# Low parts of weights issued later, and head outputs read back in place, in a one-step hybrid encoder

## The chip, the core and the metric

The kernel runs on one core of a Trainium2 chip. The metric is the device time of one execution in microseconds. Five engines work beside each other, each through its own instructions in order: TensorE (PE, matrix products), VectorE (DVE), ScalarE (ACT), GpSimd (POOL) and SyncE (SP), which here issues the transfers between memory and on-chip buffers.

## What is computed

One layer over 512 new frames and 32 frames of a running stream, T = 544 columns in all. Two groups of 16 heads (stick-breaking attention and RWKV-7) read one normalised input through one input projection; their outputs go through one output projection; a gated feed-forward part with a short convolution follows. Cut from the reference:

```python
xn = rms_norm(x, p['norm1_g'])
proj = xn @ p['w_in']
q, k, v, xr = jnp.split(proj, [D_SB, 2 * D_SB, 3 * D_SB], axis=-1)
...
o = stick_breaking(q, k_all, v_all, P)
o = rms_norm(o, p['sb_out_g'][:, None, :])
...
y_r, S_T, new_shift = rwkv7_mix(xr, shift0, S0, p)
x = x + jnp.concatenate([o, y_r.astype(x.dtype)], axis=-1) @ p['w_out']
f, new_conv = conv_ffn(rms_norm(x, p['norm2_g']), conv0, p)
x = x + f.astype(x.dtype)
```

The model is 2048 wide (16 blocks of 128 rows, k = 0 to 15), the feed-forward part 5632.

## The kernel before

**Products in three parts.** Each fp32 operand of a large product is split into a high part that TensorE takes at full rate (`hi`, made by a ScalarE cast) and the rest (`lo`, made by a VectorE subtraction that reads the cast). A product is then hi·hi + hi·lo + lo·hi. `products` (L376) issues this for one 128×128 weight block and both halves of the columns: four matmuls of 272 columns with the weight's high part, and then two with its low part.

**Weights.** They come in groups of four blocks (128×512 elements), in the order of a list `PLAN`. A group is loaded into one of 3 buffers `wr`, cast by ScalarE into one of 2 buffers `wh`, and VectorE writes its low part into one of 2 buffers `wl`. A group is 24 matmuls. `prefetch` (L313) issues casts, low parts and loads up to two groups ahead and is called after each block; `split` (L363) is called where TensorE takes the next group.

**Order of the work.** The kernel is emitted by a program that keeps an estimated clock for each engine (`clk`). While it emits the projection's matmuls, it emits pieces of the heads' side work between them (`tick`, threads) when their inputs should be there by this estimate. Every engine then carries out its own instructions in the order in which they were emitted. An engine whose next instruction waits does nothing else meanwhile.

**The start.** The 16 blocks of the input are transposed, normalised by VectorE (`xn`), cast by ScalarE (`xh`), and VectorE takes the low part (`xl`). The first two column blocks of the projection (8 weight groups: for each four k, one group for either block) are emitted by `first_products` in among this, for k = 0 to 3 once the loop over k has emitted k = 7, for k = 4 to 7 once it has emitted k = 11, and so on:

```python
    for kb in range(KB):
        if kb > 0:
            if kb + 1 < KB:
                x_high(kb + 1)
            x_low(kb)
        if kb % 4 == 3 and kb > 3:
            first_products(kb - 7)
```

**The projections** (about 57 to 985 us): 48 further column blocks of four groups each, with the heads' side work between the matmuls. Tiles of this side work that the text names are `XA`, `XB` (values and states of the RWKV chain), `AM`, `w` (general work tiles).

**The output projection.** A finished head's output goes to memory (`ocat`) and, once the last projection releases the input's tiles, `fetch` (L1435) reads it back into a `w` tile, from which `xh` and `xl` are made. Column blocks that are begun before all heads are done are kept as partial sums in memory (`pd`).

**The feed-forward part** (1200 us to the end) works mostly with products of pairs of column blocks, whose weights are split by another routine (`weights`).

Of the kernel before, what the change touches and what calls it, by code (L numbers as in the profile page):

```python
# [8 lines left out]
F32 = mybir.dt.float32  # L9
F32R = mybir.dt.float32r  # L10
BF16 = mybir.dt.bfloat16
AF = mybir.ActivationFunctionType
ALU = mybir.AluOpType
# [3 lines left out]
P = 128  # L17
# [4 lines left out]
T = SEQ + DEC  # L22
# [19 lines left out]
def hymba_step(ctx: ExitStack, tc: tile.TileContext, A: dict, O: dict):  # L42
# [19 lines left out]
    LAT = 140  # L62
    RATE = [0]
    clk = {e: 0.0 for e in COST}
# [26 lines left out]
    def stamp():  # L91
        return cur[0].ready() if cur[0] is not None else clk["PE"]

    def cols(ap):
        n = 1
        for d in ap.shape[1:]:
            n *= d
        return n
# [14 lines left out]
    V, G, AC = Engine(nc.vector, "DVE"), Engine(nc.gpsimd, "POOL"), Engine(nc.scalar, "ACT")  # L113
    act = AC.activation

    def dma(out, in_):
        if RATE[0]:
            n = cols(out) * out.shape[0] * 4
            clk["DMA"] = max(clk.get("DMA", 0.0), stamp(), clk["PE"]) + n / RATE[0]
            if cur[0] is not None:  # L120
                cur[0].rd["DMA"] = clk["DMA"] + 2300
        elif cur[0] is not None:
            cur[0].rd["DMA"] = max(clk["PE"], cur[0].ready()) + 3000
        nc.sync.dma_start(out, in_)

    def spawn(g, first=False):
        n = sum(th.first for th in threads)
        threads.insert(n if first else len(threads), Thread(g, first))
# [37 lines left out]
    def settle():  # L166
        if cur[0].ready() > clk["PE"]:
            yield


    FREE = {}
# [3 lines left out]
    def alloc(tag, shape, dtype=F32):  # L175
        after(FREE[tag].pop(0))
        pool, bufs, full = POOLS[tag]
        t = pool.tile(list(shape), dtype, tag=tag, name=nm(tag), bufs=bufs, padded_shape=full)
        OF[t.name] = tag
        return t  # L180

    def get(tag, shape=None, dtype=F32):
        while not FREE[tag]:
            yield
        t = alloc(tag, shape or POOLS[tag][2], dtype)
        yield from settle()
        return t
# [13 lines left out]
    def put(*ts):  # L201
        for t in ts:
            FREE[OF.pop(t.name)].append(stamp())
# [86 lines left out]
    raw_of, split_of = {}, {}  # L290
# [7 lines left out]
    def apart(j):  # L298
        return PLAN[j][3] in ("q", "x")

    def can_load(j):
        to = PLAN[j][3]
        return len(FREE.get("q", "")) > 1 if to == "q" else FREE["xh"] and len(FREE["xl"]) > 1 if to == "x" else FREE["wr"]
# [6 lines left out]
    def limit():  # L310
        return state["limit"] or len(PLAN)

    def prefetch():  # L313
        i = state["at"]
        while state["split"] < limit():
            j = state["split"]
            if j >= i + (QSPL if PLAN[j][3] else SPL) or not (apart(j) or FREE["wh"] and FREE["wl"]):
                break
            if state["dma"] <= j:
                if not can_load(j):  # L320
                    break
                load()
            if j > i and clk["PE"] < state[j]:
                break
            raw, ts = raw_of.pop(j)
            n = len(PLAN[j][1])
            hi, lo = ts or [alloc(t, [P, n, P], F32R) for t in ("wh", "wl")]
            AC.copy(hi, raw)
            V.tensor_tensor(lo, raw, hi.bitcast(F32), op=ALU.subtract)
            put(raw)  # L330
            split_of[j] = (hi, lo)
            state["split"] += 1
        while state["dma"] < limit():
            j = state["dma"]
            if j >= state["split"] + (QRAW if apart(j) else RAW) or not can_load(j):
                break
            load()

    def load():
        j = state["dma"]  # L340
        w, g, c0, to = PLAN[j]
        n = len(g)
        ts = None
        if apart(j):
            raw = alloc("q" if to == "q" else "xl", [P, 2 * T if to == "q" else T])
            if to == "q":
                t = alloc("q", QW, F32R)
                ts = [t[:, u * T:u * T + n * P] for u in range(2)]
            else:
                ts = [alloc(t, [P, T], F32R)[:, :n * P] for t in ("xh", "xl")]  # L350
            raw, ts[0], ts[1] = [t[:, :n * P].rearrange("p (k n) -> p k n", n=P) for t in [raw] + ts]
        else:
            raw = alloc("wr", [P, n, P])
        a = 0
        for b in range(1, n + 1):
            if b == n or g[b] != g[b - 1] + 1:
                dma(raw[:, a:b, :], w[g[a] * P:(g[b - 1] + 1) * P, c0:c0 + P].rearrange("(k p) n -> p k n", p=P))
                a = b
        raw_of[j] = raw, ts
        state["dma"] += 1  # L360
        state[j] = clk["DMA"] + 2300 if RATE[0] else clk["PE"]

    def split():  # L363
        j = state["at"]
        prefetch()
        state["at"] += 1
        return split_of.pop(j)

# [56 lines left out]
    xh, xl = [], []  # L425
# [183 lines left out]
    ocat = dr.tile([16, P, T], F32, name="ocat", bufs=1)  # L609
# [603 lines left out]
    def more_room():  # L1213
        yield from wait(SS[NP - 2], "done")
        yield from wait(SS[NP - 1], "products")
        am = yield from get("AM", None, F32R)
        ar = yield from get("AR", None, F32R)
        x = [am[:, :NC_ * P], am[:, NC_ * P:], ar]
        sp = [[x[u][:, g * 384:(g + 1) * 384] for u in (0, 2)] for g in range(2)]
        sp.append([x[1][:, u * 512:(u + 1) * 512] for u in range(2)])  # L1220
        ROOM.append((stamp(), sp))
# [210 lines left out]
        put(v)  # L1432

    spawn(more_room())
    def fetch(kb):  # L1435
        raw = yield from get("w")
        dma(raw[:, :T], ocat[kb])
        yield
        h = yield from get("xh", [P, T], F32R)
        l = yield from get("xl", [P, T], F32R)  # L1440
        AC.copy(h, raw[:, :T])
        V.tensor_tensor(l, raw[:, :T], h.bitcast(F32), op=ALU.subtract)
        put(raw)
        oh[kb], ol[kb] = h, l

    def head_done(kb):
# [3 lines left out]
    def fetch_all():  # L1450
        todo = list(range(KB))
        while todo:
            for kb in [k for k in todo if head_done(k)]:
                if kb not in oh:
                    if len(FREE["w"]) < 6:
                        break
                    spawn(fetch(kb))
                todo.remove(kb)
            yield
# [261 lines left out]
    for t in range(2):  # L1721
        for m in LAST:
            ps = getm("ps")
            for k in ALLK:
                if k % WN == 0 and t == 0:
                    kept[m, k] = split()
                hi, lo = kept[m, k // WN * WN]
# [410 lines left out]
    for t in range(2):  # L2138
        for k in range(KB):
            until(lambda: (k, t) in XN)  # L2140
            for u in range(2):
                if t == 0 and k % WN == 0:
                    sw[u, k] = split()
                hi, lo = sw[u, k // WN * WN]
# [192 lines left out]
    for gi, g in enumerate(GROUPS):  # L2337
        for m in range(LEAD):
            ps = banks(("ps", "pt")[n % 2], 2)
            for i in range(0, len(g), WN):  # L2340
                hi, lo = split()
                for q, k in enumerate(g[i:i + WN]):
                    j = k - g[0]
                    until(lambda: (gi, j // 2, 1) in HB)
                    h, l = [[HB[gi, j // 2, t][e][0][:, j % 2] for t in range(2)] for e in range(2)]
# [44 lines left out]
```

## Time and profile before

| | |
|---|---|
| median of 3 runs | 2658.87 us (2658.36 to 2659.29) |
| the profiled execution | 2658.17 us, of which 2656.3 us are the span from the first to the last instruction |
| TensorE busy | 2612.2 us, 98% of the span |
| VectorE, ScalarE, GpSimd busy | 1964.5 us (74%), 1361.4 us (51%), 241.8 us (9%) |
| DMA | 304.5 MB, mean 115 GB/s |
| mean granted TensorE clock | 0.996 of full speed |

Busy time is the time in which at least one instruction of the engine runs. TensorE's matmuls overlap each other, so its busy share tells where it stood still rather than how fast it ran. What an engine waited for is read from the idle time ahead of an instruction and from the semaphore that ended it.

### The profile page before, as it was taken

The page shows a single profiled execution, that of the slowest core. Times are in us where ns is not written, and L with a number is a line of the kernel's source. Part 1 is how long each engine was busy: PE and PEld are TensorE (multiplying, and loading weights), DVE is VectorE, ACT ScalarE, POOL GpSimd, SP SyncE. Part 2 cuts the span into 40 slices and gives each one's busy share as a digit, 9 for nine tenths or more (in the row PEclk, how much of TensorE's full clock was granted, in tenths as well). Part 3 has the DMA queues.
Part 4 walks back from the last instruction along what each step waited for, and adds up shares of the span by engine and source line. Part 5 has one row for each costly group of instructions (what it writes and reads, how often), then busy time and mean ns, then how long its engine had stood idle before and what let it go on. Part 6 is the DMA issues. An engine that isn't in the chain of part 4 may idle for free.

```text
span 2656.3 us, 54012 instructions
## 1 busy us (share of the span) xinstructions
PE 2612.2 (98%) x21546; PEld 2530.1 (95%) x21546; DVE 1964.5 (74%) x3589; ACT 1361.4 (51%) x2703; POOL 241.8 (9%) x609
## 2 busy tenths in 40 slices
PE   8999999999999999999999999999999999999999
PEld 7989988998889989999999999999999999999998
DVE  6676777676666755447788888888888897887887
ACT  5556666675666566435444444444444453443443
POOL 3210110111110100020010110101011000000000
PEclk9999999999999999999999999999999999999999
DMA  5222222232222243563334344443434364565653
GB/s 194 83 73 59 73 72 71 68 85 61 77 68 78 69 127 98 161 185 97 112 104 121 105 132 111 109 113 104 121 105 132 110 207 140 166 203 150 192 161 91
DMA packets 493237, 304.52 MB, mean 115 GB/s; under 512 B 45306, under 2 KB 458362, under 8 KB 492986
## 3 DMA queue, kind: packets, MB, share of 16 engines
q1 hardware_dynamic: 491706, 296.62, 38.8%
q0 software_dynamic: 1280, 4.46, 0.4%
q8 instruction: 169, 2.77, 0.4%
q14 instruction: 82, 0.67, 0.1%
HBM read 253.57 MB, written 47.43 MB: 113 GB/s over the span
## 4 chain that ended last, share of the span: by engine, by line
PE 64%; DVE 2%; ACT 1%; issue 0%; DMA 0%; SPq 0%; ACTq 0%; DVEq 0%
PE pt L216 27%; PE ps L216 27%; PE pj L216 9%; DVE q L109 1%; PE ps L220 0%; DVE w L109 0%; DVE wl L109 0%; ACT w L109 0%; ACT wh L109 0%; DVE xl L109 0%; ACT sp L109 0%; DMA cc<-in_cache_sb_v 0%; DVE sp L109 0%; ACT f L109 0%; DMA out_y_prompt<-f 0%
## 5 line engine op out<-in xcount | busy, mean ns | idle before, releaser
L216 PE MATMUL pj<-xh,wh 128*128 128x272 f32 x1868 | 537.4, 303 | 7.7 <-ACT wh L109 3.1
L216 PE MATMUL pj<-xl,wh 128*128 128x272 f32 x1868 | 511.8, 289 | 0.3 <-DVE xl L109 0.3
L109 DVE TENSOR_TENSOR q<-q,q 128x1024 f32<-128x1024 f32 (+7 forms) x463 | 471.0, 1038 | 6.4 <-ACT q L109 3.1
L216 PE MATMUL pj<-xh,wl 128*128 128x272 f32 x1868 | 444.0, 308 | 2.4 <-DVE wl L109 2.3
L216 PEld LDWEIGHTS pj<-xh,wh 128*128 128x128 f32 x1868 | 354.9, 190 | 20.6 <-issue 6.3
L216 PEld LDWEIGHTS pj<-xl,wh 128*128 128x128 f32 x1868 | 354.3, 190 | 4.0 <-issue 1.2
L109 DVE TENSOR_TENSOR wl<-wr,wh 128x512 fp32r<-128x512 f32 (+1 forms) x301 | 213.0, 709 | 192.7 <-ACT wh L109 186.0
L109 ACT CAST wr<-q 128x512 fp32r<-128x512 f32 (+1 forms) x301 | 180.3, 612 | 306.5 <-DVE q L109 216.9
L216 PEld LDWEIGHTS pj<-xh,wl 128*128 128x128 f32 x1868 | 302.7, 190 | 16.1 <-issue 4.5
L109 ACT CAST wh<-wr 128x512 fp32r<-128x512 f32 (+1 forms) x301 | 183.0, 610 | 165.5 <-PE pj L216 80.0
L216 PE MATMUL ps<-xh,q 128*128 128x272 f32 x922 | 241.2, 289 | 0.0
L216 PE MATMUL ps<-q,q 128*128 128x272 f32 x1160 | 237.5, 289 | 0.0
L216 PE MATMUL pt<-xh,q 128*128 128x272 f32 x1038 | 233.4, 288 | 0.0
L216 PE MATMUL pt<-q,q 128*128 128x272 f32 x844 | 215.7, 289 | 0.0
L109 DVE TENSOR_TENSOR q<-q,wr 128x512 fp32r<-128x512 f32 (+1 forms) x301 | 200.4, 674 | 0.5 <-ACT wr L109 0.4
L216 PEld LDWEIGHTS ps<-q,q 128*128 128x128 f32 x1160 | 180.9, 188 | 0.3 <-ACT f L109 0.3
L216 PEld LDWEIGHTS pt<-xh,q 128*128 128x128 f32 x1038 | 174.5, 188 | 0.0
L216 PEld LDWEIGHTS ps<-xh,q 128*128 128x128 f32 x922 | 165.3, 188 | 0.0
L109 ACT CAST q<-q 128x1024 fp32r<-128x1024 f32 (+5 forms) x197 | 147.5, 766 | 24.7 <-DVE q L109 19.0
L109 ACT CAST wh<-q 128x512 fp32r<-128x512 f32 (+1 forms) x190 | 114.1, 601 | 70.3 <-PE ps L216 34.4
L216 PEld LDWEIGHTS pt<-q,q 128*128 128x128 f32 x844 | 147.8, 188 | 0.0
L216 PE MATMUL pt<-xl,q 128*128 128x272 f32 x520 | 141.7, 289 | 0.0
(335 smaller groups left out, 6290.2 us busy)
## 6 DMA issues: line engine op xcount, KB each, us to landing
wr<-in_w_in SPq DMA_DIRECT2D x200, 256.0 KB
q<-in_w_ffn_up SPq DMA_DIRECT2D x84, 512.0 KB
q<-in_w_ffn_gate SPq DMA_DIRECT2D x80, 512.0 KB
q<-in_w_ffn_down SPq DMA_DIRECT2D x48, 512.0 KB
hd<-f SPq DMA_DIRECT2D x44, 272.0 KB
q<-hd SPq DMA_DIRECT2D x22, 544.0 KB
wr<-in_w_ffn_down SPq DMA_DIRECT2D x44, 256.0 KB
q<-in_w_ffn_down SPq DMA_DIRECT2D x24, 384.0 KB
```

What stands on the lines that cost most here:

```text
L109: return f(*a, **kw)
L216: nc.tensor.matmul(out, lhsT, rhs, start=start, stop=stop, skip_group_check=True)
```

## The change

**Low parts.** `prefetch` no longer emits a group's subtraction right behind its cast. The group is put on a list `HALF` with the time at which the estimated ScalarE clock has the cast done (plus 140 ns). At its next calls `prefetch` first runs `lows`, which emits the subtractions whose time the estimated TensorE clock has reached; `split` emits those that the group it hands out still lacks. The raw buffer is released with the subtraction, as before, so its next load moves with it.

**Fetch.** A head's output is read back into the `xl` tile in which its low part will stand (the subtraction then works in place); the `w` tile and the condition that six be free go. The cast and the subtraction are emitted in separate steps, when the estimated clocks of ScalarE and VectorE are not over 500 ns ahead of TensorE's.

```diff
--- before.py
+++ after.py
@@ -310,8 +310,20 @@
     def limit():
         return state["limit"] or len(PLAN)
 
+
+
+    HALF = []
+
+    def lows(need=-1):
+        while HALF and (HALF[0][0] <= need or HALF[0][4] <= clk["PE"]):
+            j, raw, hi, lo, _ = HALF.pop(0)
+            V.tensor_tensor(lo, raw, hi.bitcast(F32), op=ALU.subtract)
+            put(raw)
+            split_of[j] = (hi, lo)
+
     def prefetch():
         i = state["at"]
+        lows()
         while state["split"] < limit():
             j = state["split"]
             if j >= i + (QSPL if PLAN[j][3] else SPL) or not (apart(j) or FREE["wh"] and FREE["wl"]):
@@ -326,9 +338,7 @@
             n = len(PLAN[j][1])
             hi, lo = ts or [alloc(t, [P, n, P], F32R) for t in ("wh", "wl")]
             AC.copy(hi, raw)
-            V.tensor_tensor(lo, raw, hi.bitcast(F32), op=ALU.subtract)
-            put(raw)
-            split_of[j] = (hi, lo)
+            HALF.append((j, raw, hi, lo, clk["ACT"] + LAT))
             state["split"] += 1
         while state["dma"] < limit():
             j = state["dma"]
@@ -363,6 +373,7 @@
     def split():
         j = state["at"]
         prefetch()
+        lows(j)
         state["at"] += 1
         return split_of.pop(j)
 
@@ -1432,15 +1443,20 @@
         put(v)
 
     spawn(more_room())
+
     def fetch(kb):
-        raw = yield from get("w")
-        dma(raw[:, :T], ocat[kb])
+        l = yield from get("xl", [P, T], F32R)
+        raw = l.bitcast(F32)
+        dma(raw, ocat[kb])
         yield
         h = yield from get("xh", [P, T], F32R)
-        l = yield from get("xl", [P, T], F32R)
-        AC.copy(h, raw[:, :T])
-        V.tensor_tensor(l, raw[:, :T], h.bitcast(F32), op=ALU.subtract)
-        put(raw)
+        while clk["ACT"] > clk["PE"] + 500:
+            yield
+        AC.copy(h, raw)
+        yield
+        while clk["DVE"] > clk["PE"] + 500:
+            yield
+        V.tensor_tensor(l, raw, h.bitcast(F32), op=ALU.subtract)
         oh[kb], ol[kb] = h, l
 
     def head_done(kb):
@@ -1452,8 +1468,6 @@
         while todo:
             for kb in [k for k in todo if head_done(k)]:
                 if kb not in oh:
-                    if len(FREE["w"]) < 6:
-                        break
                     spawn(fetch(kb))
                 todo.remove(kb)
             yield
```

Where instructions move, at two places. The names are tiles with their numbers; `wl`, `wh`, `wr` are low part, high part and raw weights, `xn`, `xh`, `xl` the same of the input.

VectorE at the start of the kernel, behind the parameters' copy, before:

```order
L109 TENSOR_TENSOR wl_50_287<-wr_8_120,wh_49_286 128x512
L109 SCALAR_TENSOR_TENSOR xn_51_294<-xt_126,par_7_111,rsb_128 128x544
L109 TENSOR_TENSOR xl_53_298<-xn_51_294,xh_52_295 128x544
L109 TENSOR_TENSOR wl_55_301<-wr_9_122,wh_54_300 128x512
L109 SCALAR_TENSOR_TENSOR xn_58_308<-xt_126,par_7_111,rsb_128 128x544
L109 SCALAR_TENSOR_TENSOR xn_62_324<-xt_126,par_7_111,rsb_128 128x544
L109 TENSOR_TENSOR xl_64_328<-xn_58_308,xh_59_309 128x544
L109 SCALAR_TENSOR_TENSOR xn_65_330<-xt_126,par_7_111,rsb_128 128x544
L109 TENSOR_TENSOR xl_67_334<-xn_62_324,xh_63_325 128x544
```

VectorE at the same place of the changed kernel: behind the parameters' copy there come nine `xn` and eight `xl` without a weight between them, of which the last `xl` is the first row here.

```order
L109 TENSOR_TENSOR xl_80_358<-xn_75_348,xh_76_349 128x544
L109 TENSOR_TENSOR wl_50_287<-wr_8_120,wh_49_286 128x512
L109 TENSOR_TENSOR wl_55_300<-wr_9_122,wh_54_299 128x512
L109 SCALAR_TENSOR_TENSOR xn_87_421<-xt_126,par_7_111,rsb_128 128x544
L109 TENSOR_TENSOR xl_89_425<-xn_78_354,xh_79_355 128x544
L109 SCALAR_TENSOR_TENSOR xn_90_428<-xt_126,par_7_111,rsb_128 128x544
L109 TENSOR_TENSOR xl_92_432<-xn_87_421,xh_88_422 128x544
L109 SCALAR_TENSOR_TENSOR xn_93_435<-xt_126,par_7_111,rsb_128 128x544
L109 TENSOR_TENSOR xl_95_439<-xn_90_428,xh_91_429 128x544
L109 SCALAR_TENSOR_TENSOR xn_96_442<-xt_126,par_7_111,rsb_128 128x544
L109 TENSOR_TENSOR xl_98_446<-xn_93_435,xh_94_436 128x544
L109 TENSOR_TENSOR wl_82_386<-wr_10_124,wh_81_385 128x512
```

The low part of the first weight group (`wl_50`) stood ahead of the first `xn`, that of the second (`wl_55`) behind the first `xl`. Both now stand behind the eighth `xl`, and those of the third and fourth group (`wl_82` and the `wl_85` that follows the last row), which stood where `wl_50` and `wl_55` now stand, behind the twelfth.

VectorE in the projections, at the place that the trace of before has at about 188 to 194 us, before (`sp` and `ts` belong to the attention's side work, `TH` to the RWKV chain's):

```order
L109 COPY w_347_2227<-AM_343_2189 64x576 x2
L109 TENSOR_TENSOR sp_134_729<-w_323_2000,sp_134_729 64x512
L109 TENSOR_TENSOR wl_388_2404<-wr_342_2175,wh_387_2403 128x512
L109 COPY ts_379_2366<-ps_382_2379 128x128
L109 TENSOR_TENSOR sp_135_730<-w_358_2260,sp_135_730 64x2x128
L109 COPY XA_259_1555<-ps_390_2417 64x64
L109 TENSOR_TENSOR wl_395_2452<-wr_357_2256,wh_394_2451 128x512
L109 SCALAR_TENSOR_TENSOR XA_259_1555<-XA_259_1555,pc_183_1045,ps_397_2459 64x64 x2
```

The same stretch of the changed kernel:

```order
L109 TENSOR_TENSOR sp_134_727<-w_357_2260,sp_134_727 64x2x128
L109 SCALAR_TENSOR_TENSOR XA_258_1545<-XA_258_1545,pc_181_1029,ps_387_2413 64x64 x2
L109 TENSOR_SCALAR w_384_2395<-w_345_2185,m16_674 128x9x16
L109 SCALAR_TENSOR_TENSOR w_384_2395<-w_345_2185,m16_674,w_384_2395 128x9x16 x3
L109 TENSOR_TENSOR TH_330_2054<-TH_330_2054,pc_306_1908 128x1152
L109 TENSOR_TENSOR wl_386_2397<-wr_352_2229,wh_385_2396 128x512
L109 COPY XA_258_1545<-ps_396_2467 64x64
L109 TENSOR_TENSOR sp_134_727<-w_357_2260,sp_134_727 64x2x128
L109 TENSOR_TENSOR wl_398_2470<-wr_368_2304,wh_397_2469 128x512
```

Before, a `wl` stands between the two steps of the RWKV chain (`XA` copied, then updated) whose order is fixed; now they and the chain's other work stand ahead of the two `wl`, or between them. In the order in which the instructions are emitted, all but one of the 200 groups of the projections had their low part 29 large matmuls ahead of its first use (that use counted). Now 33 have it 5 ahead, that is at the `split` itself, 32 have it 11, 88 have it 17 and 47 have it 23 ahead; all eight groups of the start have it 5 ahead. All other counts (matmuls, side work) are the same; 12 fewer transfers are issued, 6 of them because 5 instead of 8 column blocks of the output projection go through memory as partial sums.

## Rows read from the trace of the kernel before

**Rows 1.** The page of the profiled execution, its first part: busy us of each engine (share of the span) and its instructions.

```profile
PE 2612.2 (98%) x21546; PEld 2530.1 (95%) x21546; DVE 1964.5 (74%) x3589; ACT 1361.4 (51%) x2703; POOL 241.8 (9%) x609
```

**Rows 2.** Busy time by stretch. Columns: the stretch in us and its length; then busy us (and instructions) of PE, PEld (weight loads of TensorE), DVE, ACT and POOL; the granted TensorE clock (1.00 is the upper of its two levels, 2.4 GHz; 0.50 the lower, 1.2 GHz); mean share of the DMA engines; GB/s. The stretches: one near the start, the projections with heads beside them, the output projection, the paired products of the feed-forward part.

```profile
21.50:31.70 10.20, 8.54 (x32) 7.50 (x33) 9.38 (x15) 5.90 (x10) 7.89 (x16) 0.50 0.94 339
...
100.00:1100.00 1000.00, 975.72 (x8642) 903.82 (x8642) 668.49 (x1463) 623.75 (x1408) 111.93 (x271) 1.00 0.27 79
1100.00:1300.00 200.00, 198.70 (x1564) 196.99 (x1563) 127.92 (x213) 85.90 (x168) 28.47 (x43) 1.00 0.50 150
1300.00:2500.00 1200.00, 1200.00 (x9543) 1199.83 (x9543) 981.23 (x1568) 534.03 (x912) 72.15 (x194) 1.00 0.46 131
```

**Rows 3.** Who waited for whom between 100 and 1100 us, of TensorE's waits and of VectorE's: the engine, the tile that it wrote and the line, what it waited for; us in total, times, longest.

```profile
PE ps L216 <- DVE XA L109: 6.6, 8, 1.8
PE ps L216 <- DVE XB L109: 3.2, 5, 1.2
...
PE pj L216 <- DVE wl L109: 2.3, 3, 1.3
...
DVE wl L109 <- ACT wh L109: 139.2, 110, 3.6
```

**Rows 4.** The timeline between 189 and 195 us, of VectorE, of ScalarE and of TensorE: start us, us, engine, line, operation, out<-in, shapes, count, and in brackets the idle time ahead and what ended it.

```profile
189.83 0.21 DVE L109 COPY XA<-ps 64x64 f32<-64x64 f32 x1
192.73 1.23 DVE L109 TENSOR_TENSOR wl<-wr,wh 128x512 fp32r<-128x512 f32 x1 [2.69 <-ACT wh L109]
193.88 0.58 DVE L109 SCALAR_TENSOR_TENSOR XA<-XA,pc,ps 64x64 f32<-64x64 f32 x2
...
190.30 1.35 ACT L109 COPY AM<-AR 64x576 f32<-64x576 f32 x2
...
192.07 0.62 ACT L109 CAST wh<-wr 128x512 fp32r<-128x512 f32 x1
...
194.62 0.46 PE L216 MATMUL ps<-XA,AM 128*128 128x128 f32 x2 [1.81 <-DVE XA L109]
```

**Rows 5.** The first and the last of the 15 TensorE stalls of over 0.25 us between 100 and 1100 us that have a VectorE wait of a `wl` in the few microseconds ahead of them, as in rows 4: each time VectorE's row and TensorE's.

```profile
182.71 0.69 DVE L109 TENSOR_TENSOR wl<-wr,wh 128x512 fp32r<-128x512 f32 x1 [2.04 <-ACT wh L109]
...
184.50 0.55 PE L220 MATMUL ps<-ident,w 128*128 128x128 f32 x3 [0.75 <-DVE w L109]
...
893.25 0.69 DVE L109 TENSOR_TENSOR wl<-wr,wh 128x512 fp32r<-128x512 f32 x1 [3.54 <-ACT wh L109]
...
894.90 0.49 PE L216 MATMUL ps<-ru,w 128*128 128x128 f32 x2 [0.36 <-DVE AM L109]
```

**Rows 6.** Two short stretches, columns as in rows 2.

```profile
195.50:198.90 3.40, 3.40 (x19) 3.40 (x18) 3.33 (x5) 1.46 (x4) 1.82 (x1) 0.52 0.19 57
...
393.50:396.90 3.40, 3.40 (x18) 3.31 (x18) 2.03 (x5) 1.04 (x4) 1.09 (x3) 0.52 0.20 56
```

**Rows 7.** The timeline of VectorE at the start, columns as in rows 4.

```profile
20.19 0.74 DVE L109 TENSOR_TENSOR wl<-wr,wh 128x512 fp32r<-128x512 f32 x1
...
22.33 0.72 DVE L109 TENSOR_TENSOR xl<-xn,xh 128x544 fp32r<-128x544 f32 x1 [0.71 <-ACT xh L109]
22.98 0.68 DVE L109 TENSOR_TENSOR wl<-wr,wh 128x512 fp32r<-128x512 f32 x1
23.58 1.47 DVE L109 SCALAR_TENSOR_TENSOR xn<-xt,par,rsb 128x544 f32<-128x544 f32 x2
...
33.25 0.71 DVE L109 TENSOR_TENSOR xl<-xn,xh 128x544 fp32r<-128x544 f32 x1
34.56 1.29 DVE L109 TENSOR_TENSOR wl<-wr,wh 128x512 fp32r<-128x512 f32 x2 [0.60 <-ACT wh L109]
```

**Rows 8.** The timeline of TensorE at the start: the first matmul, the first with a low part, one matmul of each of two weight blocks that follow each other at the lower clock and of two that lie four blocks apart at the upper, the last of the second weight group, the last of the eighth and the first of the ninth.

```profile
22.35 0.59 PE L216 MATMUL pj<-xh,wh 128*128 128x272 f32 x1 [1.70 <-ACT xh L109]
...
23.96 0.65 PE L216 MATMUL pj<-xh,wl 128*128 128x272 f32 x2
...
30.02 0.43 PE L216 MATMUL pj<-xh,wh 128*128 128x272 f32 x1
...
31.38 0.43 PE L216 MATMUL pj<-xh,wh 128*128 128x272 f32 x1
...
33.58 0.41 PE L216 MATMUL pj<-xh,wl 128*128 128x272 f32 x2
...
50.45 0.29 PE L216 MATMUL pj<-xh,wh 128*128 128x272 f32 x1
...
53.47 0.29 PE L216 MATMUL pj<-xh,wh 128*128 128x272 f32 x1
...
53.98 0.41 PE L216 MATMUL pj<-xh,wl 128*128 128x272 f32 x2
56.77 0.39 PE L216 MATMUL pj<-xh,wh 128*128 128x272 f32 x1 [2.38 <-ACT w L109]
```

**Rows 9.** The timeline of ScalarE at the start.

```profile
33.91 1.14 ACT L109 CAST wh<-wr 128x512 fp32r<-128x512 f32 x2
36.58 0.65 ACT L109 CAST xh<-xn 128x544 fp32r<-128x544 f32 x1 [1.53 <-DVE xn L109]
...
51.15 0.62 ACT L109 CAST wh<-wr 128x512 fp32r<-128x512 f32 x1 [2.36 <-PE pj L216]
```

## Prediction

> **What bounds the kernel now.** I read the page first: TensorE is busy in 2612.2 of 2656.3 us [rows 1], so it stands still for 44.1 us, and no change of order can give back more than these and what a lowered clock costs. The table by stretch says where they are [rows 2]: none between 1300 and 2500 us, 1.3 us between 1100 and 1300, 24.3 us between 100 and 1100 us, where the heads' side work runs between the projection's matmuls. Most of the rest lies in the first 57 us. The changed routine works in the projections, the output projection and the start; the feed-forward part, which takes over half the time, has nothing to gain.
>
> Then the waits. VectorE sat idle for 139.2 us, 110 times, in front of a `wl` whose cast ScalarE had not done [rows 3]. By itself that costs nothing, as VectorE is busy in two thirds of that stretch. It costs where something that TensorE wants stands behind. TensorE's largest waits there are on `XA` (6.6 us) and `XB` (3.2 us), not on `wl` (2.3 us) [rows 3], and one place shows how [rows 4]: VectorE copies an `XA` at 189.83 us, waits 2.69 us for a cast that ScalarE reaches at 192.07, behind copies of `AM`, does two `wl`, and updates `XA` at 193.88. TensorE, which wants this `XA`, stands still for 1.81 us. Of the stalls over 0.25 us in the stretch, 15 have such a `wl` wait shortly ahead; they add up to 13.7 us, the first is 0.75 and the last 0.36 us long [rows 5].
>
> One us after that stall, and once more at 393.5 us, the granted clock is at its lower level for 3.4 us, 0.52 in the rows, and comes back [rows 6]; at half speed that costs 1.7 us each time.
>
> **The change part by part.** The sum is made against the profiled execution's 2658.17 us, 0.7 under the median of the three runs.
>
> *Waits removed.* If the `wl` stand behind finished casts, the 13.7 us go, and the two spells of low clock, 3.4 us: **−17.1**. Bounds: nothing, if ScalarE is later than the estimate that defers them; 24.3 + 3.4 = 27.7 if every stall of the stretch goes.
>
> *Low parts that come too late.* Of 200 groups, 33 now have their `wl` emitted at the `split`, 5 matmuls ahead of its use. A large matmul takes 0.126 us (24 of them in 53.47 − 50.45 = 3.02 us [rows 8]), so TensorE is there after 4 × 0.126 = 0.50 us. A `wl` takes 0.69 us [rows 5], and VectorE is in the middle of something: a mean instruction of that stretch is 668.5/1463 = 0.46 us [rows 2], half of it 0.23. That leaves 0.69 + 0.23 − 0.50 = 0.42 us of stall, 33 × 0.42 = **+13.9**. The 32 with 11 matmuls have 1.26 us for the same 0.92 and cost nothing by this, and the rest less so. Bounds: nothing, where VectorE is ahead of TensorE, as it can be once nothing blocks it; and 33 × 1.27 = 42 us if each waits as long as a `wl` waited until now (139.2/110 [rows 3]). I take the middle value, since its parts are all read off rows; behind each late `wl` wait the side work's next VectorE steps.
>
> *The start.* Here the order of VectorE tells more than the stalls. Before, the first `wl` is done ahead of the first `xn`, at 20.19 us, and the second at 22.98 [rows 7]; TensorE begins at 22.35 and takes its first low part at 23.96 [rows 8]. Now nine `xn` and eight `xl` stand ahead of both. The eighth `xl` ended at 33.25 + 0.71 = 33.96 us [rows 7]; without the two `wl` in front it ends 1.3 us earlier, at 32.7, and the first `wl` at 33.3. TensorE issues four matmuls with the first high part and then waits for that, some nine us, where before it had the first two groups done at 33.99 [rows 8].
>
> From there the start is a chain, since each pair of groups waits for the next block of VectorE's `xl`. Casts need the `wh` of the group two back, as the rows of ScalarE show (a cast waits 2.36 us for TensorE at 51.15 [rows 9]), and the casts of a pair stand ahead of the next `xh` (33.91, then 36.58 [rows 9]). The steps: first pair, 44 matmuls left from 33.3 on, 5.5 us, done at T1 = 38.8. Then the fourth group's cast 0.57 [rows 9], `xh` 0.65 [rows 9], three `xl` of 0.65 and two `xn` of 0.74 in turn [rows 7], `wl` 0.69: 5.3 us, during which TensorE has four matmuls. Second pair 5.5 us: T2 = T1 + 10.9 = 49.7, with 0.1 for hand-overs. Third pair: cast 0.57, `xh` 0.65, `xl`, `xn`, `xl`, `xl` 2.7, `wl` 0.69, so 4.6, and 5.5 again: T3 = 59.9. The fourth pair has no `xl` ahead of it: 48 matmuls, 6.0 us, done at 65.9. Before it was done at 53.98 + 0.41 = 54.39 [rows 8]. That is 11.5 us later, at full clock throughout. TensorE stands still for about 9, 4.8 and 4.1 us in it. In the kernel before the clock was at 0.50 from 21.5 to 31.7 us [rows 2], after TensorE had waited 1.70 us at 22.35 and more before [rows 8], and stalls of under 2 us were followed by spells of 3.4 us [rows 6]. I count one such spell, 1.7 us, for each of the three: 5.1. Together **+16.6**. Bounds: with everything but the first wait hidden, eight groups less four matmuls from 33.3 on at 0.126 us end at 57.0, +2.6; with all of the first three pairs at the lower clock, where a matmul takes 1.36/6 = 0.227 us (31.38 − 30.02 [rows 8]), 132 × 0.10 = 13.3 on top of 11.5, +25. The 2.38 us ahead of the ninth group [rows 8] stay: they wait for the first two blocks' results to be taken away. Nothing behind can absorb the delay, since TensorE is full.
>
> *Raw buffers and loads.* A buffer is released with its `wl`, so the load of the group three later starts some two us later. It has two groups of 3 us in hand, and the DMA engines are at 0.27 [rows 2]: nothing. At the start the fourth group's load starts at 33.3 and is wanted at 38.8: hidden by the first pair.
>
> *Fetch and partial sums.* Twelve transfers and three additions on VectorE fewer, `w` tiles free earlier, casts and subtractions spread out. TensorE stands still for 1.3 us between 1100 and 1300 us [rows 2]. I count nothing, within 2 us either way; the new waits of `fetch` hold no tile that TensorE waits for.
>
> Sum: 2658.2 − 17.1 + 13.9 + 16.6 = **2671.6 us**.
>
> **A page against the rows.** The Trainium skill's page "Perfetto Trace Analysis" (Identifying the Most-Contended Engine) says that matmul busy time does not tell how far TensorE is from its limit and that weight-load busy time does. Weight loads were busy for 903.8 of 1000 us in the projections [rows 2], so by it the room there is 96 us, not 24.3. The rows speak for less: the stretch has 8642 matmuls in 1000 us, 0.116 us each, against 1200/9543 = 0.126 us where TensorE never waits [rows 2]. They are on average smaller there, which makes for shorter weight loads beside as much work. I keep 24.3 for the sum; the rule is the last of the rivals.
>
> **The rivals.**
>
> *VectorE runs ahead* (the faster side). Without 139 us of waits in its queue VectorE reaches late `wl` before TensorE does, so they cost nothing, and the other stalls go too: 2658.2 + 16.6 − 27.7 = 2647.1; with the 17.1 alone 2657.7. For it: 139.2 us are two fifths of VectorE's idle time there [rows 2, 3]. Against it: VectorE's other waits are for ScalarE and TensorE and remain. It decides for faster once waits removed less late ones exceed 16.6 + 5.3 = 21.9 us. 0.17 (0.10 faster, 0.07 level).
>
> *The start hides the rest.* The second and third wait don't occur and only +2.6 and one spell of low clock remain: 2658.2 + 4.3 − 3.2 = 2659.3. It needs the `xh` casts to pass ahead of the weights' casts; ScalarE's order has them behind. 0.08 (0.02 faster, 0.06 level).
>
> *Late low parts become the bound.* At 1.27 us each, 42 instead of 13.9: 2699.7. For it: the 33 lie in clusters, where each delays what the next one needs. 0.11.
>
> *Room inside the busy time.* If waits hide in TensorE's busy time as well, the share of `wl` in the visible stalls, 13.7/24.3, of 96.2 us is 54 us instead of 13.7: 2631. 0.04, and it is the page's rule that would have this.
>
> **How the numbers follow.** My case, a start that costs 12 to 25 us and projections that come out about level, has 0.60; its own range is 2662 to 2688. 0.2%, 5.3 us, is about what a measurement of this kernel tells from no change. Slower: 0.60 + 0.11 = 0.71. Level: 0.07 + 0.06 = 0.13. Faster: 0.10 + 0.02 + 0.04 = 0.16. The range 2653 to 2690 leaves out the last rival, the lower half of the first and most of the third, under 0.2.
>
> **What the changed profile would show.** TensorE's first low-part matmul at about 33 us instead of 23.96, waits on `wl` at some 44 and 54 us, and the ninth group at about 68 us or later instead of 56.77. VectorE's wait of `wl` on `wh` far below 139 us, waits on `XA` and `XB` smaller, waits of TensorE on `wl` well above 2.3 us between 100 and 1100 us. No stall in the feed-forward part. The prediction is wrong if the first low part comes early, if the second and third waits are missing, or if the `wl` waits of TensorE in the projections stay at 2 us.

## The result, and the profile after

The changed kernel takes 2691.18 us (median of 4 runs, 2689.76 to 2692.75) against 2658.61 us (4 runs): 1.0122 times the time before, 95% interval 1.0105 to 1.014. That is 32.6 us more; the prediction had 13.4 more. The direction was right, the time lies just above its range. The profiled execution has 2692.75 us and a span of 2691.0, 34.7 us more than the span before; the places below are read in it.

The page's first part: busy us of each engine, its share and its instructions.

```profile
PE 2618.1 (97%) x21546; PEld 2536.8 (94%) x21546; DVE 1961.7 (73%) x3584; ACT 1360.1 (51%) x2701; POOL 246.0 (9%) x609
```

TensorE is busy for 5.9 us more than in [rows 1], although it issues the same 21,546 matmuls, and it stands still for 72.9 us instead of 44.1. The second is new waiting; the first goes with more time at the lower clock (below), though no run separates it.

Who waited for whom between 100 and 1100 us, TensorE and VectorE; columns as in [rows 3].

```profile
DVE w L109 <- ACT w L109: 69.4, 56, 3.8
DVE sp L109 <- ACT sp L109: 42.8, 38, 5.4
...
PE pj L216 <- DVE wl L109: 26.9, 24, 2.8
DVE wl L109 <- ACT wh L109: 19.7, 21, 3.0
```

The change did what it says: VectorE's waits of `wl` on `wh` went from 139.2 us [rows 3] to 19.7. But VectorE did not get ahead by it. It now stands in front of the heads' own steps, `w` and `sp`, whose ScalarE halves are not done (69.4 and 42.8 us), and the `wl` stand behind these. By themselves these waits are not the loss: the fastest run below has them as well (74.0 us on `w`). The same two rows of the kernel before:

```profile
DVE w L109 <- ACT w L109: 37.8, 33, 3.4
...
DVE sp L109 <- ACT sp L109: 18.8, 22, 2.1
```

TensorE's waits for VectorE's `XA` and `XB` have left the list; in their place are 26.9 us on `wl`, which were 2.3.

By stretch, columns as in [rows 2]: three low-clock places of the start, two in the projections, the projections as a whole, one right behind the last projection, and the feed-forward part.

```profile
19.90:37.00 17.10, 6.18 (x28) 5.23 (x28) 15.41 (x24) 7.54 (x13) 9.70 (x18) 0.52 0.85 294
...
44.00:51.00 7.00, 4.67 (x20) 4.67 (x21) 4.91 (x8) 1.17 (x3) 0.00 (x0) 0.54 0.26 76
...
57.50:64.50 7.00, 5.54 (x24) 5.54 (x25) 1.99 (x4) 0.66 (x2) 4.87 (x26) 0.56 0.28 80
...
214.50:221.50 7.00, 5.15 (x23) 5.15 (x24) 4.00 (x6) 2.05 (x5) 1.53 (x4) 0.56 0.31 87
...
416.80:420.20 3.40, 3.40 (x18) 3.40 (x17) 1.88 (x4) 0.62 (x1) 0.07 (x1) 0.52 0.52 150
...
100.00:1100.00 1000.00, 967.38 (x8557) 896.50 (x8557) 668.73 (x1469) 625.14 (x1411) 120.36 (x284) 0.99 0.27 76
...
1018.00:1030.00 12.00, 9.42 (x55) 8.30 (x56) 6.76 (x15) 9.70 (x23) 0.93 (x2) 0.72 0.25 67
...
1320.00:2520.00 1200.00, 1198.03 (x9521) 1197.29 (x9521) 979.60 (x1563) 531.79 (x908) 74.11 (x202) 1.00 0.46 130
```

Between 100 and 1100 us TensorE has 8.3 us less of busy time than in [rows 2], its weight loads 7.3 less; since the changed kernel comes later, the stretch also holds 85 matmuls fewer. The 1200 us of the feed-forward part, which had no idle time in [rows 2], have 2 us of it.

TensorE at the start, columns as in [rows 8]: the last matmul ahead of each of three waits, the first behind it, and the first of the ninth group.

```profile
23.31 0.43 PE L216 MATMUL pj<-xl,wh 128*128 128x272 f32 x1
33.60 0.82 PE L216 MATMUL pj<-xh,wl 128*128 128x272 f32 x2 [9.85 <-DVE wl L109]
...
41.48 0.29 PE L216 MATMUL pj<-xl,wh 128*128 128x272 f32 x1
46.34 0.82 PE L216 MATMUL pj<-xh,wl 128*128 128x272 f32 x2 [4.57 <-DVE wl L109]
...
54.63 0.29 PE L216 MATMUL pj<-xl,wh 128*128 128x272 f32 x1
58.96 0.82 PE L216 MATMUL pj<-xh,wl 128*128 128x272 f32 x2 [4.04 <-DVE wl L109]
...
75.55 0.39 PE L216 MATMUL pj<-xh,wh 128*128 128x272 f32 x1 [2.04 <-ACT w L109]
```

These are the three waits of the prediction (9, 4.8 and 4.1 us), and the ninth group starts 18.8 us later than in [rows 8].

Two places in the projections show how a `wl` comes late now. The timeline between 340 and 347 us and between 373 and 378 us, columns as in [rows 4]; the ScalarE row ahead of each `wl` is the cast that it reads.

```profile
340.82 0.62 ACT L109 CAST wh<-wr 128x512 fp32r<-128x512 f32 x1
...
342.29 2.60 DVE L109 TENSOR_TENSOR TH<-TH,pc 128x1152 f32<-128x1152 f32 x1
...
344.81 0.57 DVE L109 SCALAR_TENSOR_TENSOR XB<-XB,pc,ps 64x64 f32<-64x64 f32 x2
...
345.41 0.44 DVE L109 TENSOR_TENSOR w<-ps,w 128x272 f32<-128x272 f32 x1
345.77 0.93 DVE L109 TENSOR_TENSOR wl<-wr,wh 128x512 fp32r<-128x512 f32 x1
...
346.75 0.52 PE L216 MATMUL pj<-xh,wl 128*128 128x272 f32 x2 [2.43 <-DVE wl L109]
...
373.73 0.61 ACT L109 CAST wh<-wr 128x512 fp32r<-128x512 f32 x1
...
374.79 0.56 DVE L109 TENSOR_TENSOR sp<-w,sp 128x384 fp32r<-128x384 f32 x1 [3.00 <-ACT sp L109]
...
375.27 0.91 DVE L109 SCALAR_TENSOR_TENSOR w<-w,par,w 128x512 f32<-128x512 f32 x2
...
376.09 0.72 DVE L109 TENSOR_TENSOR w<-w,w 128x544 f32<-128x544 f32 x1
...
376.73 0.68 DVE L109 TENSOR_TENSOR wl<-wr,wh 128x512 fp32r<-128x512 f32 x1
...
377.46 0.52 PE L216 MATMUL pj<-xh,wl 128*128 128x272 f32 x2 [2.07 <-DVE wl L109]
```

At 342 VectorE was in an instruction of 2.60 us, over five times the mean that the prediction worked with, and had an `XB` (two steps) and a `w` to do before the `wl`. At 375 it had stood still for 3.00 us in front of an `sp`, and then had three `w` to do. There are 22 stalls of over 0.25 us on a `wl` between 70 and 1008 us. In all of them the cast that this `wl` reads had ended before TensorE stopped, 1.8 to 4.6 us before the `wl` began. So none of these casts was late; the `wl` stood in VectorE's queue. In 9 of the 22 VectorE had meanwhile waited for over 1 us for other steps of ScalarE (`w`, `sp`, `XA`, `XB`), in the others it was mostly busy with work ahead of the `wl`. In three of them the `wl` itself took 1.6 to 1.9 us instead of 0.69.

How far the changed kernels lie behind the kernel before, at the same projection or output-projection matmul (counted from the first; in the kernel before the columns are at 57, 982, 1110 and 1291 us) and at the end of the span, all from the profiled executions, in us (that of the run with at least 11 was the fastest of its four, 4.0 us under their median):

| | ninth group | end of the projections | output projection begun | its end | end of span |
|---|---|---|---|---|---|
| changed kernel | +18.8 | +25.7 | +29.9 | +31.9 | +34.7 |
| start alone | +17.9 | +17.9 | +18.0 | +18.0 | +17.8 |
| all but the start | +1.0 | +9.8 | +14.2 | +16.2 | +19.2 |
| reading back alone | -0.2 | +7.9 | +7.8 | +7.2 | +5.2 |
| projections alone | +0.2 | +17.6 | +17.6 | +18.4 | +18.1 |
| the same, 5 matmuls ahead always | 0.0 | +87.2 | +87.5 | +88.2 | +88.2 |
| the same, at least 11 | -0.3 | +3.9 | +10.7 | +10.6 | +10.0 |
| the same, at least 17 | -0.1 | -7.8 | -3.4 | -2.6 | -3.9 |
| the same, at least 23 | +0.5 | -9.5 | -11.6 | -11.6 | -11.7 |

### The profile page after: what moved, and what is told of

Read it like the earlier page. It is cut to its first block, busy times and chain, and to the rows that moved or that the text cites. A ratio compares the mean times of both kernels' runs of the same rounds, so it can differ in the third digit from the quotient of the medians.

```text
span 2691.0 us, 53990 instructions
## 1 busy us (share of the span) xinstructions
PE 2618.1 (97%) x21546; PEld 2536.8 (94%) x21546; DVE 1961.7 (73%) x3584; ACT 1360.1 (51%) x2701; POOL 246.0 (9%) x609
## 4 chain that ended last, share of the span: by engine, by line
PE 88%; DVE 5%; ACT 3%; issue 1%; DMA 1%; SPq 0%; DVEq 0%; ACTq 0%
PE ps L216 33%; PE pj L216 27%; PE pt L216 26%; ACT w L109 1%; DVE w L109 1%; PE ps L220 1%; DVE wl L109 1%; DVE q L109 1%; DMA wr<-in_w_ffn_down 1%; ACT wh L109 0%; DVE sp L109 0%; ACT sp L109 0%; DMA xh<-x1d 0%; DMA out_y_prompt<-f 0%; DVE XA L109 0%
## 5 line engine op out<-in xcount | busy, mean ns | idle before, releaser
L216 PE MATMUL pj<-xh,wh 128*128 128x272 f32 x1792 | 520.2, 305 | 3.1 <-ACT w L109 2.0
L216 PE MATMUL pj<-xl,wh 128*128 128x272 f32 x1792 | 495.0, 291 | 0.2 <-DVE xl L109 0.2
L109 DVE TENSOR_TENSOR q<-q,q 128x1024 f32<-128x1024 f32 (+7 forms) x472 | 479.5, 1037 | 6.0 <-ACT q L109 2.9
L216 PE MATMUL pj<-xh,wl 128*128 128x272 f32 x1792 | 427.6, 310 | 45.9 <-DVE wl L109 45.5
L216 PEld LDWEIGHTS pj<-xh,wh 128*128 128x128 f32 x1792 | 344.2, 192 | 14.1 <-issue 5.1
L216 PEld LDWEIGHTS pj<-xh,wl 128*128 128x128 f32 x1792 | 292.5, 192 | 64.0 <-DVE wl L109 53.5
L216 PEld LDWEIGHTS pj<-xl,wh 128*128 128x128 f32 x1792 | 343.5, 192 | 3.7 <-issue 1.9
L109 ACT CAST wh<-wr 128x512 fp32r<-128x512 f32 (+1 forms) x290 | 177.4, 613 | 224.7 <-PE pj L216 131.9
L109 DVE TENSOR_TENSOR wl<-wr,wh 128x512 fp32r<-128x512 f32 (+1 forms) x290 | 203.3, 702 | 58.5 <-ACT wh L109 56.6
L109 ACT CAST q<-q 128x1024 fp32r<-128x1024 f32 (+5 forms) x206 | 152.4, 760 | 22.5 <-DVE q L109 18.5
```

The lines of the kernel that those rows point to most:

```text
L109: return f(*a, **kw)
L216: nc.tensor.matmul(out, lhsT, rhs, start=start, stop=stop, skip_group_check=True)
```

## The experiments

All are made from the changed kernel with a switch, `LATE`: where it is off, a low part is emitted with its cast, as before. "Old reading back" means that `fetch` and its caller are those of the kernel before.

**The start alone.** Deferral for the first eight groups only, old reading back.

```
+    LATE = [True]
     HALF.append((j, raw, hi, lo, clk["ACT"] + LAT))
+    if not LATE[0]:
+        lows(j)
...
+    LATE[0] = False
     for kind, p in ORDER:
```

> The reverse: the kernel before, with the low parts deferred in the start alone and the old reading back. By the chain theory first low part near 33.6 us, ninth group near 75.5 us, and a time of 2658.6 + 19 = 2677.6 us with the projections as before. If the projections make part of it good, under 2673.

2675.97 us, ratio 1.0065 (1.005 to 1.008): 17.4 us more. TensorE's three waits on `wl` up to 80 us add up to the same 18.5 us as in the changed kernel:

```profile
PE pj L216 <- DVE wl L109: 18.5, 3, 9.9
```

The delay of 17.9 us that the ninth group has stays to the end. The start chain is shown, and nothing behind absorbs it.

**All but the start.** The switch the other way round: `LATE` is off until the loop over `ORDER`, then on.

> Low parts are emitted right behind their casts until the projections begin, and deferred from there on, as in the changed kernel. If the start is a chain of its own, its whole delay goes and nothing else: the ninth group begins near 56.8 us again instead of 75.5, and the time falls by 19 us to about 2672. If part of that delay was already made good later in the changed kernel (TensorE waits less in the projections because it comes late and the side work is further on), the time falls by less than 14 us, to 2677 or more.

2676.91 us, 1.0066 (1.0051 to 1.0081): 18.3 us more than before, 14.3 less than the changed kernel, so beside late low parts some 3 us of the start's delay are made good later. The start's 17.4 and these 18.3 make 35.7, against 32.6 for both. So about half of the loss (15.2 to 18.3 us) has nothing to do with the start.

**Reading back alone.** `LATE` off throughout, `fetch` new.

> The kernel before with the new reading back of the heads' outputs alone. The changed kernel's TensorE has four stalls (4.0 us) at 1012 to 1023 us and a spell of low clock of 6.8 us behind them, between the last projection and the output projection. If these come from the new reading back, they are here too: about 4 + 3 us, 2664 to 2667. If they come from the deferred low parts (side work that ends elsewhere), this one is within 2 us of 2658.6.

2663.61 us (10 runs), 1.002 (1.001 to 1.0029): 5.1 us more, which the prediction had at 0 within 2. Until the last projections the two kernels run level. Then TensorE stands still eight times for over 0.25 us between 975 and 1130 us, 4.9 us in all (three times, 1.8 us, before) and mostly in front of side work, and runs at the lower clock for ten. The stretch from 996 to 1006 us, columns as in [rows 2]; in the kernel before the same stretch shows a clock of 1.00.

```profile
996.00:1006.00 10.00, 8.82 (x39) 7.51 (x40) 7.25 (x19) 9.71 (x25) 0.52 (x2) 0.51 0.40 108
```

**Projections alone.** `LATE` on from the loop over `ORDER` to the end of the projections, old reading back.

```
     spawn(shift_rows())
+    LATE[0] = False
```

> Low parts deferred in the projections alone; start, reading back, output projection and feed-forward part as before. If the three parts add up, this is the run with the early start less the 5.1 us of the new reading back and some 2.5 us of the feed-forward part: 2676.9 - 7.6 = 2669, with some 26 us of waits of TensorE on wl between 70 and 975 us. If the parts interfere (the reading back is dear only because low parts are late by then, say), it stays near 2672 to 2677. If the deferral itself is harmless, 2658 to 2660.

2676.45 us, 1.0069 (1.0053 to 1.0084): 18.0 us more. That is the same as with the new reading back and with low parts deferred behind the projections too, so the 5.1 us do not add. The table of delays shows why: in this run 8.3 us come at the change to the output projection (it was 9.3 us behind 90 matmuls earlier), where the low part of the last weight group but one stands on VectorE behind `xl` of the heads' outputs, and these wait for ScalarE's casts of `xh`, one of which waits 0.42 us for its load. The cast that the low part reads had long been done, at 983.19. TensorE stands still there for 4.40 us and falls to the lower clock:

```profile
982.58 0.62 ACT L109 CAST wh<-wr 128x512 fp32r<-128x512 f32 x1
...
986.58 0.72 DVE L109 TENSOR_TENSOR xl<-w,xh 128x544 fp32r<-128x544 f32 x1 [0.85 <-ACT xh L109]
...
987.65 0.73 DVE L109 TENSOR_TENSOR xl<-w,xh 128x544 fp32r<-128x544 f32 x1 [0.34 <-ACT xh L109]
988.29 0.68 DVE L109 TENSOR_TENSOR wl<-wr,wh 128x512 fp32r<-128x512 f32 x1
...
989.03 0.82 PE L216 MATMUL pj<-xh,wl 128*128 128x272 f32 x2 [4.40 <-DVE wl L109]
...
980.00:1000.00 20.00, 14.10 (x85) 12.41 (x84) 11.37 (x19) 14.11 (x29) 0.81 (x4) 0.83 0.53 185
```

With the new reading back the same change costs 4.4 us (9.8 to 14.2), and the low parts deferred behind the projections take another 5.0 (14.2 to 19.2; 0.5 here). So beside late low parts the new reading back seems to help and late low parts further on to hurt, by about as much; that is read off the delays, and no run has the new reading back with low parts deferred in the projections alone.

**Always at the split.** As the run before, but the estimate is not asked: every low part is emitted 5 matmuls ahead of its use.

```
-        while HALF and (HALF[0][0] <= need or HALF[0][4] <= clk["PE"]):
+        while HALF and (HALF[0][0] <= need or not LATE[0]):
```

> As the run before, but nothing is emitted on the estimate: all 191 low parts of the projections stand at the split, 5 matmuls ahead of their use, instead of 33. If the price is one of distance (VectorE has too few matmuls of time left), the waits of TensorE on wl grow with the count: 191 x 0.42 = 80 us by the prediction's price, 2669 - 26 + 80 = 2723 or more; 191 x 1.16 = 222 us by the price per visible stall measured in the changed kernel, 2865. If what counts is blocked side work on VectorE and ScalarE (a wl costs only where VectorE stands still just ahead of it, some 23 places), the place of the wl matters little: 2665 to 2685.

2748.07 us, 1.0336 (1.0322 to 1.035): 89.6 more. TensorE's waits on `wl`, beside which it has ten spells of low clock in the projections, 41 us in all against 6.8 (at the matmul that the kernel before has at 1110 us, 59.6 of its 87.5 us are idle time, 17.1 the clock, and 10.8 longer busy time, which was not traced):

```profile
PE pj L216 <- DVE wl L109: 81.9, 75, 4.2
```

The prediction's price of 0.42 us had 80 us for 191 of them. But it is not a price that each pays: 66 of 190 stall, by 1.21 us on average, and the others don't. And the place of the `wl` does matter: that the 23 visible places alone count is out.

**At least 11, 17 and 23 matmuls ahead.** As the run with the projections alone, but a low part that the estimate would still hold back is emitted behind the third, second or first block of the group ahead (`q >= 2`, `1` or `0`). The first run with 17 was made with the new reading back and deferral behind the projections as well.

```
     prefetch()
+    if q >= 1:
+        lows(state["at"])
```

> Low parts deferred in the projections alone, at least 11 matmuls ahead of use (73 at 11, 76 at 17, 41 at 23); the rest as before. By the prediction's own step 11 matmuls last 1.26 us and cover the 0.92 us that a late low part needs, so TensorE's waits on wl should vanish: about 2655 or less, at or below the run with at least 17. By the price per group that the runs so far show at each distance (0.24 us at 11, 0.11 at 17, 0.04 at 23) they come to 73 x 0.24 + 76 x 0.11 + 41 x 0.04 = 27.5 us, as much as with the 33 at 5 matmuls, and the time to 2665 to 2677.

> As the first of these, and in the projections and the output projection a low part that is still open when the second of the four blocks of the group ahead has been issued is emitted there, so that none stands fewer than 17 matmuls ahead of its use (5 and 11 are gone). If the time lost in the projections is that of the low parts emitted 5 (and 11) matmuls ahead, TensorE's waits for wl there (26.6 us in 23 stalls) go, and with them two or three spells of low clock: 25 to 30 us under the first of these, about 2644, and under the kernel before. If the loss comes from the new order of all the side work instead, the waits move to other tiles and the time stays within 6 us of the first of these, about 2668.

> Low parts deferred in the projections alone, but emitted at least 17 matmuls ahead of use; the rest as before. From the run with the same deadline and the new reading back (2658.3): less 5.1 for the reading back and 2.5 for the feed-forward part, 2650.7, that is 0.3% under the kernel before. If the parts interfere, 2654 to 2658.

> The same with at least 23 matmuls (the kernel before has 29). If TensorE's waits on wl shrink faster with the distance than the old waits on XA and XB come back, it is under the run with 17: 2644 to 2649. If the old waits come back with it, it lies between that run and the kernel before: 2651 to 2658. The distances are 23 in 190 of 201 groups, against 29 in the kernel before.

| at least | us | ratio, 95% interval |
|---|---|---|
| 11 | 2672.07 | 1.0053 (1.0036 to 1.007) |
| 17, reading back new, deferral to the end | 2658.27 | 0.9997 (0.9987 to 1.0006) |
| 17 | 2655.08 | 0.9984 (0.9975 to 0.9993) |
| 23 | 2646.80 | 0.9957 (0.9944 to 0.9969) |

The first run with 17 lies between its two forecasts: TensorE's idle time ahead of late low parts fell to 15.6 us and did not go. The second is 4.4 us above its main forecast, so the parts interfere. With 23 the kernel is 0.4% faster than the one before, and faster than every other run here, as forecast. Who waited for whom there between 100 and 1100 us:

```profile
DVE w L109 <- ACT w L109: 74.0, 54, 5.1
DVE wl L109 <- ACT wh L109: 73.7, 63, 3.5
...
PE pj L216 <- DVE wl L109: 8.2, 10, 2.9
...
PE ps L216 <- DVE XA L109: 2.4, 3, 1.2
```

VectorE's blocking on `wh` is halved, `XA` waits are a third of [rows 3], and the price in `wl` is 5.9 us. Behind the first matmul of the ninth group, up to the last of the projections, TensorE's stalls over 0.25 us go from 20.6 us (25) to 13.1 (15): those on a `wl` grow by 4.6 us, the others shrink by 12.1, from 18.5 to 6.4. The two spells of low clock [rows 6] are gone, as the first of the stretches below (columns as in [rows 2]) shows for the one and the second for the other. At the output-projection matmul that the kernel before has at 1110 us, by which each of these kernels has issued the same 9,047 TensorE instructions since the ninth group began, the run with 23 is 12.1 us ahead: 6.2 are idle time, 1.7 the clock (these two spells gone, one of 3.4 us new at 978 us), and 4.2 are shorter busy time, which no run explains.

```profile
195.00:205.00 10.00, 9.76 (x107) 9.10 (x106) 8.28 (x30) 6.35 (x18) 0.29 (x2) 1.00 0.34 89
395.00:405.00 10.00, 10.00 (x83) 9.29 (x84) 6.73 (x15) 5.18 (x14) 1.89 (x2) 1.00 0.26 82
```

**What a late low part costs, by its distance.** For each weight group the idle time of TensorE directly ahead of the first matmul that takes its low part, added up by the number of large matmuls between its place in the order and that matmul (groups, then us in all; the 192 groups of the projections behind the start):

| | 5 | 11 | 17 | 23 | 29 |
|---|---|---|---|---|---|
| before | | | | | 192, 2.2 |
| changed kernel | 33, 16.5 | 29, 7.0 | 84, 1.9 | 45, 0.9 | 1, 0 |
| all but the start | 30, 16.5 | 32, 7.4 | 81, 1.9 | 47, 0.9 | 2, 0 |
| projections alone | 32, 22.5 | 31, 7.4 | 80, 1.9 | 47, 0.9 | 2, 0 |
| always at the split | 190, 82.2 | | | | 2, 0 |
| at least 11 | | 73, 22.3 | 76, 5.4 | 41, 0 | 2, 0 |
| at least 17 | | | 137, 15.6 | 53, 1.1 | 2, 0 |
| at least 23 | | | | 190, 7.0 | 2, 0 |

That is 0.43 to 0.70 us each at 5 (the 0.70 has the one stall of 4.40 us in it), 0.23 to 0.31 at 11, up to 0.11 at 17, up to 0.04 at 23 and 0.01 at 29. The counts of 32, 88 and 47 that are given with the change take in a few groups of the output projection. The run with at least 11 came out as its second forecast had it, 27.7 us of idle time against 27.5, though by more at 11 and less at 17 and 23.

## Why the prediction was wrong in size

In the profiled executions the sum was short by 21.3 us (34.7 against 13.4): 2.2 of them lie in the start, 10.1 in the projections and 9.0 behind them.

**The start: right.** Predicted +16.6, measured 17.4 for it alone and 18.8 at the ninth group of the changed kernel. First low part at 33.60 (33.3 predicted), waits of 9.85, 4.57 and 4.04 us (9, 4.8, 4.1). The chain of VectorE's `xn` and `xl` was the right reading. A little short was the clock: one spell of 3.4 us for each wait was counted, and the rows have 0.52 over 17.1 us with 28 matmuls, and 0.54 and 0.56 over 7 us each with 20 and 24. At the prediction's 0.10 us for each of these 72 that is about 7 us instead of 5.1.

**The late low parts: the step that failed.** The 33 at 5 matmuls were to cost 13.9 us and cost 16.5, which is close. But "the 32 with 11 matmuls have 1.26 us for the same 0.92 and cost nothing by this, and the rest less so" is wrong: they cost 7.0, and those at 17 and 23 another 2.8. Together 26.3, less the 2.2 of before: +24.1 instead of +13.9. The lateness was worked out as a mean, one `wl` and half a mean instruction. It is no such thing: most low parts are on time, and some are two to three us late, because VectorE is in a long instruction or has waited for ScalarE's other steps. The mean came out near, over the 33 and again over the 190 of the run at the split (0.43), but it says nothing on what a little more distance saves. The run with at least 11 tests this step: TensorE's idle time ahead of low parts should have vanished and was 27.7 us, the time should have been about 2655 or less and was 2672.07. Not all of that time is this step in the projections: of its delay of 10.0 us, 6.8 come at the change to the output projection.

**Waits removed: the stalls right, the clock wrong.** Stalls that are not on `wl`, over 0.25 us in the same stretch (behind the first matmul of the ninth group, up to the last of the projections), fell from 18.5 to 0.8 us: -17.7, predicted -13.7. (At the place of [rows 4] VectorE does one `wl`, of 1.23 us, and not two.) The 3.4 us of low clock were to go too. They did not, as the new stalls take the place of the old: the lower level shows for 6.8 us at 214.5 and 3.4 at 416.8, 10.2 instead of 6.8, which costs 1.7 more instead of 3.4 less. By these terms the projections lose 24.1 - 17.7 + 1.7 = 8.1 us; the delay grew by 25.7 - 18.8 = 6.9 there, predicted -3.2. The 1.2 between the two were not traced; the kernels don't have the same side work behind them at the same projection matmul.

**Behind the projections: not seen.** Predicted nothing; measured 34.7 - 25.7 = 9.0 us. Of that 4.2 come at the change to the output projection, where TensorE waits for side work and falls to the lower clock (the stretch from 1018 us), and 4.8 behind it. "No stall in the feed-forward part" was wrong: there are five of over 0.25 us up to the end of the span, 3.2 us against 1.0, as here (columns as in [rows 4]):

```profile
2194.24 0.39 PE L216 MATMUL pt<-xl,wh 128*128 128x272 f32 x1 [0.80 <-ACT wh L109]
...
2196.14 0.52 PE L216 MATMUL pt<-xl,wl 128*128 128x272 f32 x2 [1.14 <-DVE wl L109]
```

The idle time of a part in the kernel before (none) bounds what can be gained there, not what a changed order can lose. The runs place the 4.8 us with the low parts deferred behind the projections: 0.5 us in the run that has them only in the projections, 5.0 in the one that has them to the end and the new reading back too, which alone gains 2.6 there (7.8 to 5.2). TensorE's stalls over 0.25 us behind that point agree: 6.7 us in the changed kernel against 1.8 before, 6.5 with all but the start, 2.7 with the projections alone, 1.3 with the reading back alone. The reading back, put at 0, is worth 5.1 us of loss alone; in the changed kernel it can't be told apart from these, and start and projections alone already make 17.4 + 18.0 = 35.4, more than the 32.6 of the whole.

**The rivals.** "VectorE runs ahead" fell: its idle time moved to `w` and `sp`. "Late low parts become the bound" named the right direction, by half: 26 of its 42 us, through some of the groups at every distance and not through 1.27 us for each of the 33. "The start hides the rest" fell with the three waits. "Room inside the busy time" is not found at its size, and not wholly excluded: up to the matmul at 1110 us, with the same TensorE instructions, the time that is neither idle nor the clock's shrinks by 2.8 us in the changed kernel, by 5.5 with at least 17 and by 4.2 with 23, which halves VectorE's blocking, against the 40 more that the rival wanted. Why it shrinks is open. That the removed stalls went because VectorE is blocked less, and not because a TensorE that waits for `wl` leaves the side work more time, is argued and not shown; in the run with 23, 4.6 us more on `wl` go with 12.1 us less elsewhere.

## What to carry to other kernels

Deferring a step on an in-order engine so that it need not wait moves the wait to whatever stands there next; look for who waits behind that before counting the wait as gone. Price the slack that a deferred step keeps by the spread of the engine's lateness (its longest instructions, its longest waits for others), not by its mean: here a third of the low parts were late with 5 matmuls of slack and a few of 190 with 23, and the version that gave up only one block of slack was the one that gained most. A part without idle time bounds a gain, not a loss.

## What the runs showed of the hardware that was not expected

A stall of TensorE does not always bring the clock down. In the changed kernel 2.79 us of waiting at 213.6 us were followed by 6.8 us at the lower level and 2.18 us at 413.5 by 3.4, but the stalls of 2.43 and 2.07 us at 344.3 and 375.4 us by none (1.00 in both stretches, columns as in [rows 2]):

```profile
346.00:356.00 10.00, 9.25 (x73) 9.09 (x74) 6.27 (x14) 5.42 (x14) 0.15 (x1) 1.00 0.24 65
377.00:387.00 10.00, 9.54 (x82) 9.39 (x84) 4.69 (x12) 5.50 (x13) 0.41 (x3) 1.00 0.28 79
```

At the start the level stayed low for 17.1 us, most of it while TensorE waited; so of a long spell only the matmuls in it cost, 28 here.
